# Splitting the mixer's weight units with ScalarE copies and an adding DMA in place of GpSimd

## The chip, the cores and the metric

The kernel runs on one core of a Trainium2 chip. The metric is device time in microseconds (us) of one execution; lower is better. One core has TensorE (matmuls; PE in the profile, its weight loads PEld), VectorE (DVE), ScalarE (ACT), GpSimd (POOL) and SyncE (SP, which here only issues DMAs).

## The reference

A decoder trunk of two layers over 512 tokens of width 1024, in float32:

```
for i in range(DEPTH):                                   # 2 layers
    h = 0.5 * swiglu(x, ffn1_w_gate[i], ffn1_w_up[i], ffn1_w_down[i])      # width 2752
    x = layer_norm(DEEPNORM_ALPHA * x + h, ...)
    h = hybrid_mixer(x, w_in[i], ..., w_out[i])
    x = layer_norm(DEEPNORM_ALPHA * x + h, ...)
    h = 0.5 * swiglu(x, ffn2_...)
    x = layer_norm(DEEPNORM_ALPHA * x + h, ...)
    x = x + sigmoid(x @ ple_w_gate[i] + ple_b_gate[i]) * (p[i] @ ple_w_proj[i])
```

The mixer projects x with w_in, runs three groups of attention heads and multiplies their concatenated outputs with w_out. The groups are: four NSA heads (a compressed branch over blocks of keys, and a window branch and a selected-block branch, which at 512 tokens are plain causal softmaxes), four differential heads (two causal softmaxes each, the second subtracted from the first with a factor), and eight FoX heads (a causal softmax with a decay term).

## The kernel before

**Split operands.** Every large product is made from split operands: a float32 matrix a is kept as hi + lo, where hi is a rounded to the reduced form (F32R) that TensorE multiplies in one pass, and lo = a - hi. A product then is three matmuls: hi·hi, hi·lo, lo·hi. Activations are split when they are made (`hilo`); weights are split on the fly.

**Weight units.** All weights lie in DRAM as one stream of units of 128x1024 floats (512 KB), in the order in which they are used. `_load` brings a unit into one of two raw buffers by a DMA on SyncE's queue (`opt["raw"]` is 2). `_split` makes two tiles: hi by a ScalarE copy (L218), and lo by a subtraction raw - hi (L219). The raw buffer is free for the next load when lo is done. The unit's tag, made in `unit_tags`, says which group of buffers holds hi and lo: "w" (six buffers), "p" or "h". A second letter P sends the subtraction to GpSimd instead of VectorE. The tag "wR" is for units used without a split.

**Which units go to GpSimd.** In each layer's mixer these are the sixteen projection units (`cmp`, `q0`, `q1`, `kk`, the four differential heads Gd0 to Gd3 and the eight FoX heads Gf0 to Gf7; tag "wP"), and six of the eight units of w_out (three "wP", three "pP"). With two layers that makes 44. All other units, 298 of them, are subtracted on VectorE.

**How far ahead.** `unit()` hands out a unit and calls `ahead`, which emits the split of the units up to two further on (`lead_mx` is 2). Their hi and lo need buffers, which come free when TensorE has finished with an earlier unit.

**The mixer's order.** The order of the steps is written by hand in the string `SEQ`. G is a head's projection, Q its scores and softmax (`softmax`: row maximum on VectorE at L733, exponential on ScalarE at L735, scaling by the reciprocal sum on VectorE at L743 or, for the second softmax of a differential head, L747), T the transposition on TensorE with the split of the result (L757, L241, L242), P the product with the values, W a piece of w_out. Within each engine the framework puts the instructions in its final order; it follows the program's order and its own reckoning of when each is ready.

**Names in the profile.** raw is a loaded unit, whi and wlo its two parts, ps a PSUM tile, P a softmax's matrix, sst its maxima and sums, oT the split output of a head pair, VF the FoX values, raw_r and rot the rotary embedding's tiles, gx and gy those of the compressed branch's activation function. L249 is the line of every matmul, L241 and L242 those of every activation split.

Of the kernel before, what the change touches and what calls it, by code (L numbers as in the profile page):

```python
# [19 lines left out]
F32 = mybir.dt.float32  # L20
F32R = mybir.dt.float32r
AF = mybir.ActivationFunctionType
ALU = mybir.AluOpType
# [144 lines left out]
class _Body:  # L168
    def __init__(self, tc, A, out, pools, opt):
        self.tc, self.nc, self.A, self.out, self.opt = tc, tc.nc, A, out, opt  # L170
        self.cp, self.rawp, self.sp, self.tp, self.mp, self.pp, self.Pp, self.op, self.dp = pools
        self.tags = unit_tags()
        self.dma_u = self.split_u = self.use_u = 0
        self.n_units = A["ws"].shape[0]
        self.rawt, self.hl = {}, {}
        self.lead = 3
        self.pending = []
        self.st = {}
# [29 lines left out]
    def _split(self, u):  # L208
        while self.dma_u <= u:
            self._load(self.dma_u)  # L210
            self.dma_u += 1
        r = self.rawt.pop(u)
        tag = self.tags[u]
        if tag.endswith("R"):
            self.hl[u] = r
            return
        hi, lo = self.big(tag[0], name="whi"), self.big(tag[0], name="wlo")
        self.nc.scalar.activation(hi, r, AF.Copy)  # L218
        (self.nc.gpsimd if self.opt["pool"] and tag[1:] else self.nc.vector).tensor_sub(lo, r, hi.bitcast(F32))  # L219
        self.hl[u] = hi, lo  # L220

    def ahead(self, n):
# [810 lines left out]
def unit_tags():  # L1033

    rest = 2 * NFULL + 1 + 2 * (NFULL // 2 + 1) - 3
    ffn = ["p"] * 3 + ["w"] * rest
    mix = ["p"] * 3 + ["w"]
    for n in SEQ:
        if n == "VF":
            mix += VFT  # L1040
        elif n[0] == "h":
            mix += [PHT[int(n[2])]]
        elif n[0] == "G" or n in ("cmp", "q0", "q1", "kk"):
            mix += ["w" if n in DVE_LO else "wP"]
    mix += ["wP"] * 3 + ["pP"] * 3 + ["w"] * 2
    ffn2 = ["h", "h", "h"] + ["w"] * rest
    ple = ["p"] * 2 + ["h"] * 8
    return (ffn + mix + ffn2 + ple) * L
# [50 lines left out]
```

## Time and profile before

| | |
|---|---|
| runs, median (lowest to highest of 3) | 2171.5 us (2169.47 to 2177.97) |
| the profiled execution's own time | 2160.23 us |
| its span, first to last instruction | 2158.5 us |
| TensorE busy | 2122.6 us (98%) |
| VectorE busy | 1034.2 us (48%) |
| ScalarE busy | 820.4 us (38%) |
| GpSimd busy | 151.5 us (7%) |

By stage, in us of the span:

| stage | length | TensorE busy | VectorE | ScalarE | GpSimd | granted clock |
|---|---|---|---|---|---|---|
| layer 1, first FFN (0 to 366) | 366 | 363.5 | 138.7 | 112.7 | 3.2 | 1.00 |
| layer 1, mixer (366 to 634) | 268 | 256.4 | 189.3 | 171.4 | 64.0 | 0.98 |
| end of w_out (634 to 670) | 36 | 35.7 | 30.5 | 12.4 | 4.0 | 1.00 |
| second FFN, embedding, next first FFN (670 to 1434) | 764 | 763.1 | 289.3 | 222.9 | 6.7 | 1.00 |
| layer 2, mixer (1434 to 1702) | 268 | 254.9 | 189.4 | 168.7 | 62.8 | 0.97 |
| the rest (1702 to the end) | 457 | 449.0 | 197.1 | 132.4 | 10.8 | 1.00 |

Matmuls are pipelined, so a stretch in which TensorE is busy all the time is not one in which it runs at its best rate; its idle time is a lower bound of what it loses. The granted clock is the share of TensorE's full clock that it had. The idle time of an engine that nobody waits for costs nothing.

### The profile page before, as it was taken

How to read it: one execution, taken by the hardware profiler on the slowest of the kernel's cores; microseconds unless marked ns; L12 is line 12 of the kernel's file. 1: busy time of each engine (PE TensorE's matmuls, PEld its weight loads, DVE VectorE, ACT ScalarE, POOL GpSimd, SP SyncE). 2: the span in 40 equal slices, each digit the busy share in tenths (PEclk: the TensorE clock that was granted, in tenths of full speed). 3: DMA queues.
4: the chain of work that ended last, by engine and by line, in shares of the span. 5: the costliest groups of instructions: out<-in, count | busy, mean ns of one | idle time of the engine just before them, and what ended most of it. 6: DMA issues, size and time to landing. Idle time of an engine off the chain costs nothing.

```text
span 2158.5 us, 25961 instructions
## 1 busy us (share of the span) xinstructions
PE 2122.6 (98%) x10135; PEld 1760.1 (82%) x10135; DVE 1034.2 (48%) x1777; ACT 820.4 (38%) x1372; POOL 151.5 (7%) x114
## 2 busy tenths in 40 slices
PE   9999999999999999999999999999999999999999
PEld 7888888787778888888888888887877788888877
DVE  4333336378875333335623333363788753333355
ACT  5222213457753222213422222143577532222132
POOL 0000001222220000000000000012212200000000
PEclk9999999999999999999999999999999999999999
DMA  6333334442341332334223323343323413333331
GB/s 205 97 98 98 108 107 154 128 149 77 111 154 59 98 98 97 116 100 129 96 67 95 95 97 106 109 161 120 123 94 103 163 60 98 97 98 116 99 129 67
DMA packets 76107, 236.07 MB, mean 109 GB/s; under 512 B 11344, under 2 KB 13520, under 8 KB 75984
## 3 DMA queue, kind: packets, MB, share of 16 engines
q1 hardware_dynamic: 74864, 230.74, 33.7%
q0 software_dynamic: 1120, 3.67, 0.4%
q8 instruction: 80, 1.31, 0.2%
q14 instruction: 43, 0.35, 0.0%
HBM read 209.46 MB, written 6.29 MB: 100 GB/s over the span
## 4 chain that ended last, share of the span: by engine, by line
PE 87%; DVE 6%; ACT 3%; DMA 2%; issue 1%; SPq 0%; DVEq 0%; ACTq 0%
PE ps L249 84%; PE ps L757 2%; DMA raw<-in_ws_dram 2%; ACT whi L218 1%; DVE wlo L219 1%; PE ps L266 1%; DVE P L733 0%; DVE P L743 0%; DVE x L303 0%; DVE P L747 0%; DVE oT L242 0%; ACT P L735 0%; DVE PT L242 0%; DVE raw_r L541 0%; DVE lnu L302 0%
## 5 line engine op out<-in xcount | busy, mean ns | idle before, releaser
L218 ACT ACTIVATE whi<-raw 128x1024 fp32r<-128x1024 f32 x342 | 362.0, 1060 | 1042.2 <-PE ps L249 674.0
L219 DVE TENSOR_TENSOR wlo<-raw,whi 128x1024 fp32r<-128x1024 f32 x298 | 363.9, 1223 | 606.4 <-ACT whi L218 605.8
L249 PE MATMUL ps<-xh,wlo 128*128 128x512 f32 (+1 forms) x1688 | 644.7, 382 | 0.0
L249 PE MATMUL ps<-xh,whi 128*128 128x512 f32 (+1 forms) x1688 | 643.7, 382 | 1.0 <-ACT xh L268 0.8
L249 PE MATMUL ps<-xl,whi 128*128 128x512 f32 (+1 forms) x1688 | 644.5, 382 | 0.0
L249 PE MATMUL ps<-whi,h 128*128 128x512 f32 x1376 | 427.2, 389 | 0.0
L249 PEld LDWEIGHTS ps<-xh,whi 128*128 128x128 f32 x1688 | 317.2, 188 | 61.0 <-ACT xh L268 1.5
L249 PEld LDWEIGHTS ps<-xh,wlo 128*128 128x128 f32 x1688 | 318.1, 188 | 58.5 <-DVE wlo L219 0.3
L249 PEld LDWEIGHTS ps<-xl,whi 128*128 128x128 f32 x1688 | 317.8, 188 | 58.8 <-DVE xl L269 0.6
L249 PEld LDWEIGHTS ps<-whi,h 128*128 128x128 f32 x1376 | 258.0, 188 | 53.1
L249 PE MATMUL ps<-wlo,h 128*128 128x512 f32 x704 | 274.1, 389 | 0.0
L335 DVE TENSOR_TENSOR hraw<-silu,ps 128x512 f32<-128x512 f32 x88 | 60.5, 688 | 291.5 <-PE ps L249 290.6
L249 PEld LDWEIGHTS ps<-wlo,h 128*128 128x128 f32 x704 | 132.1, 188 | 27.6
L219 POOL TENSOR_TENSOR wlo<-raw,whi 128x1024 fp32r<-128x1024 f32 x44 | 107.1, 2434 | 285.4 <-ACT whi L218 204.1
L735 ACT ACTIVATE P<-P,sst 128x128 f32<-128x128 f32 x192 | 106.5, 558 | 21.7 <-DVE sst L733 21.2
L249 PE MATMUL ps<-whi,xh 128*128 128x512 f32 (+2 forms) x264 | 99.3, 379 | 3.5 <-DVE VF L467 3.4
L298 POOL TENSOR_TENSOR mv<-mv,mhalf 128x1 f32<-128x1 f32 x24 | 23.0, 958 | 1099.6 <-DVE mv L297 1099.6
L249 PE MATMUL ps<-wlo,xh 128*128 128x512 f32 (+2 forms) x264 | 99.3, 377 | 0.0
L249 PE MATMUL ps<-whi,xl 128*128 128x512 f32 (+2 forms) x264 | 99.0, 376 | 0.0
L733 DVE CUSTOM_DVE_ANT_0 P<-ps,mask 128x128 f32<-128x128 f32 x192 | 88.9, 488 | 19.8 <-PE ps L249 16.7
L249 PE MATMUL ps<-whi,oT 128*128 128x512 f32 x256 | 86.0, 403 | 6.1 <-ACT oT L241 3.0
L242 DVE TENSOR_TENSOR PT<-ps,PT 128x512 fp32r<-128x512 f32 (+1 forms) x120 | 67.6, 592 | 14.6 <-ACT PT L241 14.1
(194 smaller groups left out, 1902.4 us busy)
## 6 DMA issues: line engine op xcount, KB each, us to landing
raw<-in_ws_dram SPq DMA_DIRECT2D x342, 512.0 KB
wraw<-in_ws_dram SPq DMA_DIRECT2D x16, 512.0 KB
dx<-x SPq DMA_DIRECT2D x8, 512.0 KB
x<-dx SPq DMA_DIRECT2D x8, 512.0 KB
rot<-raw_r SPq DMA_DIRECT2D x28, 128.0 KB
bc<-in_ln_g_dram SPq DMA_DIRECT2D x6, 512.0 KB
bc<-in_ln_b_dram SPq DMA_DIRECT2D x6, 512.0 KB
xraw<-in_xt_dram SPq DMA_DIRECT2D x8, 256.0 KB
```

The source lines that it names most:

```text
L218: self.nc.scalar.activation(hi, r, AF.Copy)
L219: (self.nc.gpsimd if self.opt["pool"] and tag[1:] else self.nc.vector).tensor_sub(lo, r, hi.bitcast(F32))
L242: nc.vector.tensor_sub(lo, src, hi.bitcast(F32))
L249: self.nc.tensor.matmul(out, l, r, start=start, stop=stop, skip_group_check=loose)
L266: nc.tensor.transpose(p[:, j], self.x[t][:, 128 * k:128 * k + 128], self.ident)
L298: nc.gpsimd.tensor_tensor(mv[:, 3:4], mv[:, 2:3], self.mhalf, op=ALU.pow)
L335: nc.vector.tensor_mul(r[0:n], s[up:up + n], pu[up:up + n])
L733: nc.vector.tensor_tensor_reduce(v, p[:, 0:n], self.mask[:, 512 - n:512], -scale, 3e38, ALU.add, ALU.min, nm[:, t:t + 1])
L735: nc.scalar.activation(v, v, AF.Exp, bias=nm[:, t:t + 1], scale=-1.0, accum_out=sm[:, t:t + 1])
L757: nc.tensor.transpose(p[:, 128 * i:128 * i + 128], P[:, off[t] + 128 * kb:off[t] + 128 * kb + 128], self.ident)
```

## The change

For a unit whose tag has the second letter P, lo is no longer raw - hi on GpSimd. ScalarE writes the negated raw, rounded to F32R as hi is, into lo, that is -hi; then a DMA issued by GpSimd adds raw to it in place. lo is then raw - hi, as before. The three "pP" units of w_out in each layer become "p", so VectorE subtracts them. So 38 units (19 a layer) go the new way, and six move from GpSimd to VectorE. Below the change the kernel's lines are five further down.

```diff
         hi, lo = self.big(tag[0], name="whi"), self.big(tag[0], name="wlo")
         self.nc.scalar.activation(hi, r, AF.Copy)
-        (self.nc.gpsimd if self.opt["pool"] and tag[1:] else self.nc.vector).tensor_sub(lo, r, hi.bitcast(F32))
+        if tag[1:]:
+
+            self.nc.scalar.activation(lo, r, AF.Copy, scale=-1.0)
+            self.nc.gpsimd.dma_start(lo.bitcast(F32), r, accum_op=ALU.add)
+        else:
+            self.nc.vector.tensor_sub(lo, r, hi.bitcast(F32))
         self.hl[u] = hi, lo
...
-    mix += ["wP"] * 3 + ["pP"] * 3 + ["w"] * 2
+    mix += ["wP"] * 3 + ["p"] * 3 + ["w"] * 2
```

## Rows read from the trace of the kernel before

**Rows 1.** Busy time of each engine in the two mixer stretches: the stretch, its length, then for PE, PEld, DVE, ACT and POOL the busy us and the number of instructions, the granted clock, the DMA engines' share and GB/s.

```profile
366.00:634.00 268.00, 256.44 (x1375) 211.11 (x1374) 189.26 (x488) 171.40 (x393) 64.00 (x42) 0.98 0.41 129
1434.00:1702.00 268.00, 254.88 (x1361) 210.50 (x1359) 189.44 (x485) 168.70 (x389) 62.82 (x43) 0.97 0.38 119
```

**Rows 2.** The waits of TensorE over the whole span: who waited, for whom, us in total, times, the longest.

```profile
PE ps L249 <- DVE sst L733: 6.5, 5, 2.4
PE ps L757 <- ACT P L735: 4.8, 2, 2.4
PE ps L249 <- DVE VF L467: 3.4, 2, 2.4
...
PE ps L249 <- DVE oT L242: 2.9, 2, 1.4
...
PE ps L713 <- DVE sc L706: 2.0, 2, 1.0
...
PE ps L249 <- DVE gx L648: 0.6, 1, 0.6
```

**Rows 3.** From timelines of VectorE and GpSimd in the mixers: start, duration, engine, line, operation, tiles, shape, how many are merged, and in brackets the engine's idle time before it and what ended it.

```profile
457.94 1.27 DVE L743 TENSOR_SCALAR P<-P,sst 128x128 f32<-128x128 f32 x4
478.64 3.09 DVE L743 TENSOR_SCALAR P<-P,sst 128x128 f32<-128x128 f32 x4
514.29 3.37 DVE L743 TENSOR_SCALAR P<-P,sst 128x128 f32<-128x128 f32 x4
512.02 0.69 DVE L242 TENSOR_TENSOR oT<-pair,oT 128x512 fp32r<-128x512 f32 x1
621.35 2.38 DVE L242 TENSOR_TENSOR oT<-pair,oT 128x512 fp32r<-128x512 f32 x1 [0.70 <-ACT oT L241]
620.82 2.36 POOL L219 TENSOR_TENSOR wlo<-raw,whi 128x1024 fp32r<-128x1024 f32 x1 [0.71 <-ACT whi L218]
391.24 2.51 DVE L541 TENSOR_TENSOR raw_r<-raw_r,rope 128x512 f32<-128x512 f32 x1 [2.46 <-DMA rot<-raw_r]
1463.83 2.73 DVE L541 TENSOR_TENSOR raw_r<-raw_r,rope 128x512 f32<-128x512 f32 x1 [2.62 <-DMA rot<-raw_r]
1467.19 2.77 DVE L543 TENSOR_TENSOR raw_r<-raw_r,rot 128x512 f32<-128x512 f32 x1
1540.88 3.27 DVE L645 TENSOR_SCALAR gy<-gy 128x64 f32<-128x64 f32 x1
```

**Rows 4.** From the page's costliest groups: the two parts of a weight unit's split, with count, busy us, mean ns of one, idle time before and what ended it.

```profile
L218 ACT ACTIVATE whi<-raw 128x1024 fp32r<-128x1024 f32 x342 | 362.0, 1060 | 1042.2 <-PE ps L249 674.0
L219 DVE TENSOR_TENSOR wlo<-raw,whi 128x1024 fp32r<-128x1024 f32 x298 | 363.9, 1223 | 606.4 <-ACT whi L218 605.8
...
L219 POOL TENSOR_TENSOR wlo<-raw,whi 128x1024 fp32r<-128x1024 f32 x44 | 107.1, 2434 | 285.4 <-ACT whi L218 204.1
```

**Rows 5.** Short stretches after waits of TensorE, columns as in rows 1; the granted clock is the third number from the end.

```profile
517.00:523.00 6.00, 5.08 (x25) 4.55 (x26) 5.49 (x17) 3.79 (x11) 0.70 (x2) 0.72 0.39 112
...
622.00:630.00 8.00, 6.57 (x22) 5.02 (x21) 5.72 (x6) 2.75 (x3) 1.18 (x1) 0.79 0.83 293
1472.00:1479.00 7.00, 6.59 (x22) 5.29 (x23) 0.95 (x2) 0.11 (x1) 0.00 (x0) 0.76 0.26 102
1544.00:1557.00 13.00, 12.77 (x55) 11.85 (x56) 7.30 (x29) 6.31 (x20) 0.10 (x1) 0.61 0.13 45
```

**Rows 6.** From the chain of work that ended last, the exponentials right behind the copy at 593.07 (start, us, what); and from the timelines of GpSimd and ScalarE around Gd3's split (columns as in rows 3).

```profile
594.40 1.91 ACT P L735 x6
...
537.20 2.40 POOL L219 TENSOR_TENSOR wlo<-raw,whi 128x1024 fp32r<-128x1024 f32 x1 [5.16 <-PE ps L249]
...
533.69 1.36 ACT L241 ACTIVATE PT<-ps 128x512 fp32r<-128x512 f32 x3
```

**Rows 7.** DMA issues: tiles, queue, operation, count, KB each, median us from issue to landing (for two kinds that GpSimd issues); and one load of a raw unit in the chain of work (start, us, what).

```profile
rope<-in_rope_dram POOLq DMA_DIRECT2D x8, 256.0 KB, 4.6
...
ptraw<-in_pt_dram POOLq DMA_DIRECT2D x4, 256.0 KB, 3.2
...
380.26 3.60 DMA raw<-in_ws_dram
```

**Rows 8.** From timelines, the split and the first use of lo: q1 in layer 1 (GpSimd's start, TensorE's first matmul with wlo), q1 in layer 2, Gf3 in layer 1 (ScalarE's copy, TensorE's first matmul with wlo), the third unit of w_out in layer 1.

```profile
428.53 2.40 POOL L219 TENSOR_TENSOR wlo<-raw,whi 128x1024 fp32r<-128x1024 f32 x1 [7.44 <-PE ps L249]
435.62 0.39 PE L249 MATMUL ps<-xh,wlo 128*128 128x512 f32 x1
1503.99 2.40 POOL L219 TENSOR_TENSOR wlo<-raw,whi 128x1024 fp32r<-128x1024 f32 x1 [7.44 <-PE ps L249]
1512.43 0.39 PE L249 MATMUL ps<-xh,wlo 128*128 128x512 f32 x1
441.36 1.05 ACT L218 ACTIVATE whi<-raw 128x1024 fp32r<-128x1024 f32 x1
452.22 0.48 PE L249 MATMUL ps<-xh,wlo 128*128 128x512 f32 x1
593.07 1.05 ACT L218 ACTIVATE whi<-raw 128x1024 fp32r<-128x1024 f32 x1
603.96 0.40 PE L249 MATMUL ps<-wlo,oT 128*128 128x512 f32 x1
```

**Rows 9.** The waits of SyncE's DMA queue over the whole span, columns as in rows 2.

```profile
SPq L205 <- POOL wlo L219: 146.6, 34, 17.4
```

## The prediction

> **What bounds the kernel now.** I read the busy time by stage first: in both mixer stretches TensorE is busy 256.4 and 254.9 of 268 us, VectorE about 189 (71%), ScalarE about 170 (64%), and the granted clock is 0.98 and 0.97; outside them TensorE stands at 98% or more with clock 1.00 (the table above). So the changed units lie in the only two stretches where TensorE has idle time to give back [rows 1]. Next, who TensorE waits for [rows 2]: the reader is to see that the waits on VectorE there add up to 6.5 + 3.4 + 2.9 + 2.0 + 0.6 = 15.4 us, and that the largest one on ScalarE, 4.8 us, is for the exponentials. Then why VectorE is late [rows 3]. The same four L743 operations take 1.27 us in one place, and 3.37 and 3.09 us where GpSimd's subtraction runs; one oT subtraction takes 0.69 us alone and 2.38 us beside a GpSimd subtraction that began 0.53 us earlier; rope's raw_r 2.51, 2.73 and 2.77 us; a 128x64 operation 3.27 us. The long oT ends 0.55 us after GpSimd's operation, about its own clean length: the two engines do not run such operations side by side, and the one that comes second stands still. Each of the long ones stands right before a TensorE wait of [rows 2].
>
> **What is removed.** 44 GpSimd subtractions of 2434 ns [rows 4], 22 a layer, and with them the hold on VectorE. GpSimd's own 107 us were no bound (7% of the span). Going through [rows 2] in order:
> - sst (the row maxima before a softmax), 6.5 us in 5 waits. Two are 1.8 each, behind the L743 run of 3.37 us and its twin in layer 2; the run loses 3.37 - 1.27 = 2.1, more than the wait. One of 2.4 follows the 3.27 us operation. Together 6.0; the two others are 0.2 each and are left.
> - VF, 3.4 us: 1.0 in layer 1, 2.4 in layer 2. Rope loses 2.51 - 0.68 = 1.8 in layer 1, and (2.73 + 2.77) - 2 x 0.68 = 4.1 in layer 2 (0.68 estimated from oT's 0.69, same shape). All could go, but in layer 1 ScalarE gets a second copy here (below), so 2.9.
> - sc, 2.0: the L743 run before it is late by 3.09 - 1.27 = 1.8 against 1.0 a layer: all 2.0.
> - gx, 0.6: gone.
> - oT at the end of the mixer, 2.9: the operation loses 1.7, but VectorE now subtracts for the last w_out unit at just this moment (1223 ns), so I take half, 1.4.
>
> Sum 12.9 us. TensorE that is early runs into waits that have not moved (the exponentials, 4.8), so I keep three quarters: **-9.7**. Bounds: 0, if every later wait takes it back, and 14.9.
>
> **The clock.** After four of these waits the granted clock is on its lower level, 1.2 instead of 2.4 GHz, for a while; the mean over each stretch is 0.72, 0.79, 0.76 and 0.61 [rows 5]. One minus the mean, times the length: 1.7, 1.7, 1.7 and 5.1 us, in sum 10.1. The one at 622 has a ScalarE wait in front of it too, and whether a shorter wait still drops the clock no row says. I take half, **-5.0**; bounds 0 and 10.1.
>
> **What is added on ScalarE.** 38 negated copies, 19 a layer, of the shape of L218's copies, 1060 ns [rows 4]: 40 us in all, in stretches where it is busy 64%. A copy delays what stands behind it until ScalarE's next idle moment; followed one by one through its queue, only two a layer reach the chain of waits. The unit at 593.07 has the exponentials of a differential head right behind it (1.91 us on the chain [rows 6]): 1.06 a layer, **+2.1**. The one before rope's q0 leaves about 0.5 us, taken off at VF above. The other seventeen are hidden by idle time of ScalarE waiting for TensorE or VectorE; without that cover all 38 cost 40. The negated copy doesn't wait for the first one, only for raw and for its buffer.
>
> **What is added on VectorE.** Six subtractions of 1223 ns, 7.3 us, in place of six GpSimd ones. The first of a layer comes earlier than GpSimd's (1.2 instead of 2.4), the second waits for a buffer while VectorE is idle, the third was counted at oT. Otherwise nothing.
>
> **What is added on the DMA.** 38 adding transfers on GpSimd's queue, each 512 KB of raw onto 512 KB in place. No row shows one. Before, lo stood about 3.5 us after the first copy began; now it stands after two copies (2.1) and D, the time from the issue to the landing. Lower bound for D: GpSimd's loads of 256 KB land after 3.2 to 4.6 us [rows 7]; upper bound: an add reads 1 MB and writes 512 KB, three times what such a load reads and writes, so 13.8 if all of the 4.6 grew with the bytes. The nearest is between GpSimd's 4.6 for half the bytes and the 3.6 of a raw load of 512 KB [rows 7]; I add about 2 for the second operand and take 6.5. The Trainium skill ("DMA: Bandwidth & Descriptors", Anatomy of one DMA — SWDGE (gpsimd) path) fits a GpSimd-issued DMA as 2.0 us plus bytes at 436 GB/s: an estimate of 3.2 us for 512 KB, 4.4 for two operands. For 256 KB that fit gives 2.6 where the rows have 3.2 and 4.6; by it the late term that follows is 0 instead of 0.5.
>
> Who waits for lo, in the tightest places [rows 8]: q1's buffer comes free at 428.53, its copy would end at 429.59, and TensorE reads lo at 435.62: margin 6.0; in layer 2 1512.43 - 1505.05 = 7.4. Gf3: 452.22 - (441.36 + 2.12) = 8.7. The third w_out unit: 603.96 - (593.07 + 2.12) = 8.8. Gf3 of layer 2 has 11.7; the third w_out unit there 8.8 again; all others have more. At D = 6.5 only q1 of layer 1 is late: **+0.5**.
>
> The raw buffer is also given back some 5 us later, so the load that waits for it stands longer at the head of SyncE's queue (146.6 us behind GpSimd now [rows 9]). Behind it wait rope's moves and those of the FoX heads, and for these the next head's scores. The raw itself has slack: at the tightest, Gd0's buffer is back at 461.05 + 2.1 + 6.5 = 469.7, the load takes 3.6, and the next copy from it begins at 476.15. **+1.0**, bounds 0 and 4 (a 2 us delay once a layer). GpSimd's other work (the copies at L788) has slack of several us.
>
> **Sum.** -9.7 - 5.0 + 2.1 + 0.5 + 1.0 = -11.1; the framework orders the queues anew, which I set at nothing. The profiled execution took 2160.2 us (span 2158.5), so 2149.1; it lay 11.3 below the median of the runs, 2171.5, and against that I forecast **2160.4**, 0.51% faster. A change under 0.5%, 10.9 us, can't be told from none.
>
> **Rivals.**
> *The add lands late.* Place: q1, Gf3 and the third w_out unit. With D above the margins the price is (D - 6.0) + (D - 8.7) + (D - 8.8) in layer 1 and (D - 7.4) + (D - 8.8) in layer 2: 5D - 39.7. The other terms are -11.6, so it decides from D = 10.3; at 13 (and 1.3 more for Gf3 of layer 2) it is 26.6, giving 2171.5 + 15.0 = 2186.5. For it: the add has three times the bytes of the load that took 4.6; against it: a raw load of 512 KB takes 3.6. Chance 0.13, of which 0.10 slower by over 0.5%.
> *ScalarE stands at the buffer.* GpSimd waited for lo's buffer behind the first copy; now ScalarE does, and what is queued behind the copy waits too. In layer 1 the waits were 3.8 (q1), 3.4 (537.20 after a copy that ended at 533.7 [rows 6]), 2.1 and 1.0 us; 20.6 over both layers. If all is on the path: -11.1 + 20.6 = +9.5, and with the copies of these units themselves, 1.06 each, four a layer, +18.0: 2189.5. It decides from 11.1 of these. For it: PT copies began right behind at 533.69. Against: at q1 ScalarE had nothing to do, and the framework can put ready work first. Chance 0.11, of which 0.08 slower.
> *The relief is swallowed, or doesn't come.* VectorE is early, but TensorE then waits for the exponentials, the clock falls anyway, and a GpSimd that issues transfers holds VectorE as its subtraction did. Terms: 0 + 0 + 2.1 + 0.5 + 1.0 = +3.6 at one end, half the gains (-3.7) at the other: 2168 to 2175. Chance 0.16, nearly all no change (0.02 faster).
> *The add waits for VectorE.* L743's runs and GpSimd's work exclude each other, and the order can turn: an issue behind a clean run starts 1.27 us late, D = 7.8, q1 late by 1.8 and 0.4: 2162. Chance 0.04, no change. The Trainium skill states that as a trap ("SBUF — State Buffer", SBUF: two separate sides): while VectorE runs a two-port operation, GpSimd cannot write descriptors. No run here shows it yet.
>
> **Range and chances.** Forecast, 0.56; its own range 2150 (nearly all waits kept) to 2168: 0.42 faster by over 0.5%, 0.14 not. If both the waits and the clock come back whole and cost nothing, 14.9 + 10.1 = 25: 2146.5, the low end. The high end takes in the slower rivals up to D = 13: 2186. Faster 0.42 + 0.02 = 0.44; slower 0.10 + 0.08 = 0.18; the rest, 0.38, the same.
>
> **What the profile after would show.** A run of four L743 operations at 1.3 us and oT at 0.7; TensorE's waits on sst, VF, sc and gx gone; fewer stretches under clock 1.00; ScalarE 40 us busier; no TensorE wait for lo. Wrong would be: a wait of matmuls on the adding DMA, exponentials late behind copies, or the same clock.

## Result and the profile after

| | median of the runs | its runs | profiled execution: time, span, TensorE busy |
|---|---|---|---|
| before | 2170.5 us | 2169.4 to 2178.0 (4) | 2160.2, 2158.5, 2122.6 us |
| after | 2149.2 us | 2147.4 to 2155.9 (4) | 2147.4, 2145.7, 2116.4 us |

The changed kernel is faster: 0.9909 of the time before, 95% interval [0.9888, 0.9930]. Two later comparisons with more runs give less: 0.9939 [0.9923, 0.9955] and 0.9949 [0.9924, 0.9973], medians 12.6 and 13.2 us apart. Profile against profile it is 12.8 us; the profiled execution of after is the fastest of its four, that of before is faster than all four of its row.

First the two mixer stretches, columns as in [rows 1], whose answer this is:

```profile
366.00:634.00 268.00, 256.23 (x1390) 210.43 (x1389) 180.86 (x495) 189.12 (x412) 27.66 (x39) 0.99 0.62 167
1434.00:1702.00 268.00, 260.28 (x1404) 214.68 (x1403) 183.63 (x499) 190.70 (x414) 28.19 (x40) 0.99 0.61 168
```

In the same 268 us TensorE gets through 15 and 43 more matmuls, with the clock at 0.99. ScalarE is 18 and 22 us busier, GpSimd 36 and 35 less, and the DMA engines' share rises from 0.41 and 0.38 to 0.62 and 0.61. Then TensorE's waits over the whole span, the answer to [rows 2]:

```profile
PE ps L762 <- ACT P L740: 4.7, 2, 2.3
...
PE ps L254 <- DMA fa<-fa: 2.5, 2, 2.1
PE ps L254 <- ACT fb L566: 1.7, 2, 0.9
...
PE ps L254 <- DVE VF L472: 1.3, 1, 1.3
...
PE ps L254 <- DMA wraw<-in_ws_dram: 1.3, 1, 1.3
...
PE ps L254 <- DMA fa<-ct: 0.7, 2, 0.3
PE ps L254 <- DVE sst L738: 0.4, 2, 0.2
```

The five waits on VectorE that made up 15.4 us are down to 2.0 (VF 1.3, sst 0.4, and 0.3 for g, where gx was). In their place stand some new ones: 2.5 + 0.7 for moves of the FoX heads and 1.3 for a weight load, all issued by SyncE, 1.7 for a ScalarE result (fb), and 0.9 for VectorE's osq. No matmul waits for an add. Whole span: TensorE's idle time went from 2158.5 - 2122.6 = 35.9 us to 2145.7 - 2116.4 = 29.3, 6.6 less, and its busy time fell by 6.2 with the same 10135 matmuls; less busy time for the same matmuls is the clock's part.

Why VectorE is no longer late is read from its groups kept apart by shape (line, operation, shape, count | busy us, mean ns of one | idle before). Three groups of before, with all their instructions, then the same ones of after:

```profile
L242 DVE TENSOR_TENSOR oT<-pair,oT 128x512 fp32r<-128x512 f32 x16 | 14.9, 929 | 2.1 <-ACT oT L241 2.1
...
L541 DVE TENSOR_TENSOR raw_r<-raw_r,rope 128x512 f32<-128x512 f32 x14 | 13.5, 961 | 12.8 <-DMA rot<-raw_r 12.8
...
L743 DVE TENSOR_SCALAR P<-P,sst 128x128 f32<-128x128 f32 x16 | 8.2, 511 | 0.3
```

```profile
L247 DVE TENSOR_TENSOR oT<-pair,oT 128x512 fp32r<-128x512 f32 x16 | 11.0, 687 | 0.7 <-ACT oT L246 0.7
...
L546 DVE TENSOR_TENSOR raw_r<-raw_r,rope 128x512 f32<-128x512 f32 x14 | 9.6, 686 | 16.0 <-DMA rot<-raw_r 9.4 <-ACT whi L218 6.7
...
L748 DVE TENSOR_SCALAR P<-P,sst 128x128 f32<-128x128 f32 x16 | 4.5, 283 | 0.3
```

The long ones of [rows 3] are gone from the mean: 929 to 687 ns, 961 to 686, 511 to 283. GpSimd's subtraction did not hold every operation of VectorE, though. In before, PT<-ps,PT (128x512), which reads PSUM, took 687 ns at the median in the 17 cases beside one and 681 in the other 63; rope's raw_r<-raw_r,rope, all in SBUF, took 2.51 and 2.73 us beside one and 0.69 in the other 12. So what the change frees are VectorE's operations within SBUF.

The split's own parts, the answer to [rows 4] and [rows 7] (the last line is a DMA issue: count, KB each, median us from issue to landing):

```profile
L221 ACT ACTIVATE wlo<-raw 128x1024 fp32r<-128x1024 f32 x38 | 40.1, 1055 | 7.3 <-PE ps L254 7.3
...
L222 POOL DMA_DIRECT2D wlo<-raw x38 | 33.2, 874 | 316.0 <-ACT wlo L221 238.2 <-PE ps L809 25.4 <-ACT gy L649 19.9
...
wlo<-raw POOLq DMA_DIRECT2D x38, 512.0 KB, 5.0
```

An add lands 5.0 us after its issue (4.4 to 7.6), and the issue takes GpSimd 0.87 us. SyncE's loads behind such units wait about as long as before, the answer to [rows 9]:

```profile
SPq L205 <- DMA wlo<-raw: 133.3, 29, 10.8
```

### The profile page after: what moved, and what is told of

Read it like the earlier page. It is cut to its first block, busy times and chain, and to the rows that moved or that the text cites. A ratio compares the mean times of both kernels' runs of the same rounds, so it can differ in the third digit from the quotient of the medians.

```text
span 2145.7 us, 26020 instructions
## 1 busy us (share of the span) xinstructions
PE 2116.4 (99%) x10135; PEld 1754.9 (82%) x10135; DVE 1008.9 (47%) x1783; ACT 854.2 (40%) x1410; POOL 78.5 (4%) x108
## 5 line engine op out<-in xcount | busy, mean ns | idle before, releaser
L224 DVE TENSOR_TENSOR wlo<-raw,whi 128x1024 fp32r<-128x1024 f32 x304 | 371.9, 1224 | 611.9 <-ACT whi L218 606.6
L762 PE MATMUL ps<-ident,P 128*128 128x128 f32 x400 | 64.6, 282 | 6.1 <-ACT P L740 4.7
L246 ACT ACTIVATE PT<-ps 128x512 fp32r<-128x512 f32 (+1 forms) x120 | 58.5, 523 | 16.1 <-PE ps L762 12.4
```

Of the source, the lines that this page charges most:

```text
L224: self.nc.vector.tensor_sub(lo, r, hi.bitcast(F32))
L246: nc.scalar.activation(hi, src, AF.Copy)
L762: nc.tensor.transpose(p[:, 128 * i:128 * i + 128], P[:, off[t] + 128 * kb:off[t] + 128 * kb + 128], self.ident)
```

## Experiments

The kernels ran in three sets, each on a chip of its own together with runs of before; so a kernel's time is compared with before of its own set, and times across sets are good for a rough comparison only. Each execution comes with its span and mean granted clock. I split the mean over a kernel's executions in two: span times (1 - clock), what the clock's lower level took, and the rest of the span. The clock is given to three places, so one execution's split is good to 1 us. The rest is the steadier part: before has 2145.5, 2146.2 and 2145.5 in the three sets, and 16.1, 20.5 and 16.7 lost to the clock.

| kernel | median, us | ratio to before, 95% interval | lost to the clock | the rest |
|---|---|---|---|---|
| first set: before | 2163.0 (26 runs) | | 16.1 | 2145.5 |
| before, built again | 2168.1 (10) | 1.0027 [1.0004, 1.0049] | 18.6 | 2147.5 |
| after | 2150.3 (10) | 0.9939 [0.9923, 0.9955] | 8.8 | 2140.1 |
| after, GpSimd reading again | 2177.7 (5) | 1.0071 [1.0043, 1.0098] | 16.5 | 2159.4 |
| only w_out's six units | 2163.5 (10) | 0.9983 [0.9955, 1.0011] | 15.6 | 2142.4 |
| second set: before | 2168.5 (15) | | 20.5 | 2146.2 |
| only ScalarE's second copies | 2171.3 (10) | 1.0010 [0.9998, 1.0023] | 12.8 | 2156.5 |
| all 44 by the adding DMA | 2159.0 (6) | 0.9954 [0.9937, 0.9970] | 8.6 | 2148.3 |
| the add issued twice | 2224.3 (4) | 1.0255 [1.0230, 1.0280] | 38.9 | 2183.2 |
| cmp, kk, q1 on VectorE | 2146.9 (4) | 0.9900 [0.9882, 0.9918] | 7.0 | 2138.0 |
| third set: before | 2164.1 (27) | | 16.7 | 2145.5 |
| after | 2150.9 (12) | 0.9949 [0.9924, 0.9973] | 10.6 | 2139.5 |
| cmp, kk, q1 on VectorE | 2146.3 (6) | 0.9918 [0.9887, 0.9949] | 3.6 | 2139.6 |
| and Gf0, Gf1 | 2147.2 (10) | 0.9924 [0.9902, 0.9947] | 4.7 | 2140.9 |
| all 44 on VectorE | 2172.9 (12) | 1.0043 [1.0022, 1.0064] | 28.2 | 2142.2 |

**The measure itself: before, built again, and after.** No edit.

> The kernel before once more, for a second profile of it. If its profiled execution (2160.2 us, 11 below the median of its runs) was a lucky one, this one shows a span of 2165 to 2175 and more of TensorE's half clock than the 27 us of the first; if the first was typical for the code, 2157 to 2161 with the same six stretches of half clock.

> The changed kernel once more. 2147 to 2152 us timed; a profile that differs from its first by a stretch of half clock at most (3.4 us of it cost 1.7 us).

The same kernel built again differs from itself by 0.27% and its interval leaves out 1. So a single difference of under about 0.3%, 6 us, is not told from none here. Of the change's 12.6 us in this set, 7.3 are the clock's and 5.4 the rest; in the third set 6.1 and 6.0.

**Bring the hold back without the subtraction's result.** After each add GpSimd also computes raw - hi, into a tile that nobody reads (scr, scrp in the profile):

```diff
-            self.nc.gpsimd.dma_start(lo.bitcast(F32), r, accum_op=ALU.add)
+            d = self.nc.gpsimd.dma_start(lo.bitcast(F32), r, accum_op=ALU.add)
+            for c in (slice(0, 512), slice(512, 1024)): self.after(self.nc.gpsimd.tensor_sub(self.scr, r[:, c], hi.bitcast(F32)[:, c]), d)
...
-        nc.vector.memset(self.mhalf, -0.5)
+        nc.vector.memset(self.mhalf, -0.5); self.scr = self.cp.tile([128, 512], F32, name="scrp")
```

> The changed kernel, and GpSimd also subtracts, into a scratch tile, for the same 38 units right after it has issued the add. lo does not depend on it. Theory (GpSimd's subtraction held VectorE): the waits on sst, VF and sc come back, about 11 us of the 15 in the first profile of before, with half clock behind them: 2160 to 2172 us. Rival (the framework's new order of the queues made the gain): the order is nearly that of the changed kernel, so 2147 to 2153. Rival (the six units moved to VectorE made it): 2147 to 2155 too.

The gain is gone and more: 27 us over the changed kernel, and 5.7 over the highest time that was expected. VectorE's and GpSimd's groups by shape in this kernel:

```profile
L548 DVE TENSOR_TENSOR raw_r<-raw_r,rot 128x512 f32<-128x512 f32 x14 | 14.7, 1051 | 0.2
...
L546 DVE TENSOR_TENSOR raw_r<-raw_r,rope 128x512 f32<-128x512 f32 x14 | 13.3, 953 | 14.9 <-DMA rot<-raw_r 14.9
...
L645 DVE TENSOR_TENSOR gy<-gx 128x64 f32<-128x64 f32 x4 | 4.2, 1054 | 0.0
...
L222 POOL TENSOR_TENSOR scrp<-raw,whi 128x512 f32<-128x512 f32 x76 | 113.6, 1495 | 2.8
```

Two of rope's operations are at 0.95 and 1.05 us instead of 0.69, one of 128x64 at 1.05, and TensorE waits 6.7 us for sst (0.4 in after) and 3.3 for sc (none in after). No other engine uses what GpSimd computes here, so it is GpSimd's running that does this, and not the queues' order, which the rival would have kept. Nor is it the raw buffer: SyncE's loads wait 137.1 us for adds here and 133.3 in after, TensorE 0.4 for an add. The hold falls on other operations than in before: oT (128x512) and L748's 128x128 operations are at their clean lengths here, 686 and 283 ns on the mean, so the wait on sst has come back by other operations. Why it overshoots stays open. VectorE is held no longer than in before: without its weight subtractions it is busy 30.0 us more than in after, before 33.3 us more. The Trainium skill ("SBUF — State Buffer", SBUF: two separate sides) calls the ports that VectorE and GpSimd share an exclusive lock, held for a whole instruction. The rows agree: oT 929 ns on the mean before and 687 after.

**One part alone: w_out's six units.** The kernel before with the new tags.

```diff
-    mix += ["wP"] * 3 + ["pP"] * 3 + ["w"] * 2
+    mix += ["wP"] * 3 + ["p"] * 3 + ["w"] * 2
```

> Only the tags of w_out's six units are changed; the 38 others are subtracted by GpSimd as before. Theory: what this part gives is the oT wait at the end of each mixer, 1.4 to 2.9 us in all, and perhaps a stretch of half clock (1.7): 2165 to 2170 us. Rival (the six units made most of the gain): 2150 to 2158.

In its trace the wait on oT at VectorE (2.9 us) is gone, and sst (9.2), VF (3.1) and sc (2.0) remain. That is the step "oT" by itself. Its time, 0.5 us over before and 4.6 under before built again, can't be told from none; it lies 1.5 under the range expected. Its rest is 3.1 us under before's (2142.4 against 2145.5), as much as the wait that went (2.9), and more than half of after's 5.4.

**The other part alone: all 44 units by the adding DMA.** w_out's last three stay "pP".

```diff
-    mix += ["wP"] * 3 + ["p"] * 3 + ["w"] * 2
+    mix += ["wP"] * 3 + ["pP"] * 3 + ["w"] * 2
```

> All 44 units go the new way, w_out's last three of a layer as well (they stay pP). Theory: the first of them is needed at once (before, GpSimd's lo ended at 611.28 and TensorE reads the unit from 611.0); copy, copy and add end 7.1 us after the first copy began at 607.76, so 3 to 4 us late in each layer, and half clock behind that: 2155 to 2164. Rival (it doesn't matter who makes the last three): 2147 to 2153.

It is 9.5 us under before of its set, three quarters of the whole change's 12.6 and 13.2, and all of it is the clock's (20.5 to 8.6 us); the rest is 2.1 over before. TensorE waits 4.8 us for whi and 2.0 for VectorE's wlo at the end of w_out, which neither kernel does. One line of ScalarE there, with its idle time:

```profile
640.28 2.19 ACT L218 ACTIVATE whi<-raw 128x1024 fp32r<-128x1024 f32 x2 [8.69 <-DMA raw<-in_ws_dram]
```

Three units in a row on the add keep both raw buffers, the next two loads are late, and with them w_out's last units. So the two parts of the change need each other: by the rest, 2148.3 against after's 2140.1 and 2139.5 in the other sets, VectorE's three subtractions a layer are worth some 8 us once the others go by DMA. After did not run in this set, so that is a comparison across sets.

**The second copies alone.** The kernel before, with ScalarE's negated copy into lo ahead of GpSimd's subtraction, which overwrites it; units tagged "wP" only.

```diff
+        if tag == "wP": self.nc.scalar.activation(lo, r, AF.Copy, scale=-1.0)
         (self.nc.gpsimd if self.opt["pool"] and tag[1:] else self.nc.vector).tensor_sub(lo, r, hi.bitcast(F32))
```

> The kernel before, and ScalarE also writes the negated copy into lo for the 38 units; GpSimd's subtraction then overwrites it. So ScalarE's part of the change is there, the hold on VectorE stays, no add. Theory (the copies fall into ScalarE's idle time but for the one before the exponentials): 2 us more without the clock's part, 2165 to 2171 timed. Rival (ScalarE is nearly the bound, 40 us of copies show): 2180 or more.

In sum they cost 2.8 us, which the interval can't tell from none: 38 copies don't cost 40. But this is a net of two things, 10.3 us more of the rest and 7.7 less of the clock's, since the framework orders the queues anew and other waits come up (gy 7.3 us, and x at 4.7 where before has 2.6). So it excludes the 29 us that the rival adds (20.6 of waits and 8.5 of copies) and does not measure the copy's own price. It also shows that the clock's part doesn't follow the hold alone: GpSimd subtracts here as before, and 7.7 us less are lost to the clock.

**How late may the add be?** It is issued twice, so lo is 2 raw - hi.

```diff
             self.nc.gpsimd.dma_start(lo.bitcast(F32), r, accum_op=ALU.add)
+            self.nc.gpsimd.dma_start(lo.bitcast(F32), r, accum_op=ALU.add)
```

> The changed kernel with the add of raw issued twice, the second waiting for the first; lo is then 2 raw - hi, which is not the split. lo lands about 10 us after the first issue instead of 5. Theory (margins of 6.0, 7.4, 8.7 and 8.8 at q1, Gf3 and the third w_out unit): 5 x 10 - 39.7 = 10 us of waits for lo, and the raw buffers and SyncE's queue 5 us later on top: 2158 to 2170. Rival (the framework's order hides a later lo): within 3 of the changed kernel.

Measured: 55.8 us over before of its set, so some 70 over after, about seven times the waits that were expected. TensorE's waits in this kernel:

```profile
PE ps L254 <- DMA wlo<-raw: 17.9, 10, 3.2
PE ps L254 <- DVE sst L738: 10.7, 8, 4.4
PE ps L254 <- ACT raw_r L543: 6.6, 2, 3.5
PE ps L254 <- DMA fa<-ct: 5.7, 2, 5.1
PE ps L254 <- ACT fb L566: 5.6, 4, 3.1
PE ps L254 <- ACT whi L218: 4.4, 3, 2.4
```

Only 17.9 us are lo itself, in ten places where I had counted five. Of the others, some stand behind a raw load in SyncE's queue, which issues in order; I followed one of them. The queue there (start, us, what):

```profile
590.08 0.48 SPq L558 DMA_DIRECT2D fb<-fb  x1
595.09 0.33 SPq L205 DMA_DIRECT2D raw<-in_ws_dram  x1
595.51 1.15 SPq L558 DMA_DIRECT2D fa<-ct  x1
```

The load stands until 595.09 for a buffer that the add still reads, the move of fa behind it is issued at 595.51, and the product that needs it starts at 600.35, 3.5 us late (the profile names no releaser for this wait; that it is the move goes by the order). That all the others have this cause is not shown. The second part is the clock: 38.9 us lost to it, against 8.8 and 10.6 in after. So, across sets, some 43 us are in the rest and 28 to 30 are the clock's.

**Units back to VectorE: three, then five.** Twice, the second time beside after and a version with two more.

```diff
-DVE_LO = ()
+DVE_LO = ("cmp", "kk", "q1")
```

> The changed kernel, but cmp, kk and q1 are subtracted by VectorE, which is busy 9 of 40 us there (400 to 440). Their raw buffers come back about 5 us earlier, so SyncE's queue is free for the FoX heads' moves. Theory: the waits on fa (2.1 and 0.5 us) and on wraw (1.3) of the changed kernel go: 2145 to 2148. Rival (those waits have another cause, and VectorE's 3.7 us more per layer show): 2150 or more.

> The changed kernel once more, beside the two versions below on one chip. Theory and rival alike: 2147 to 2152 us, 0.7 to 1.0% under the kernel before.

> cmp, kk and q1 split by VectorE, the other 32 units by the adding DMA. In the first look at it TensorE's wait for q0's moves (fa<-fa, 2.1 and 0.5 us) was gone, but it waited 1.1 and 0.9 us for Gf3's lo on the add. Theory: the moves wait at SyncE behind loads whose buffer the adds give back late, and VectorE's own split gives it back earlier, so it is 2 to 3 us under the changed kernel: 2145 to 2149. Rival: the difference between the two was one of the two calls they ran in; then they are within 1 us.

```diff
-DVE_LO = ()
+DVE_LO = ("cmp", "kk", "q1", "Gf1", "Gf0")
```

> Gf0 and Gf1 go back to VectorE as well, so 28 units are left on the adding DMA. Theory: Gf3's buffer and rope's q0 no longer stand behind ScalarE's second copies, so the waits on VF (1.3 us) and on Gf3's add (1.0 us a layer) go too: 1 to 3 us under the version with three, 2143 to 2147. Rival: VectorE is late again in rope and the values of the FoX heads, where it has 2.4 us of subtractions more a layer: 0 to 4 us over the version with three.

Beside after, in the third set, the version with three is 4.6 us faster, and the two intervals overlap; in the second set, without after beside it, it has 0.9900 of before's time, where after had 0.9939 and 0.9949 in its sets. So it beats before, and after by no more than the same kernel differs from itself. In the first of its two traces the waits for fa<-fa and for the weight load are gone; in the second 0.9 us of fa<-fa is left. But in the third set, beside after, its rest is that of after (2139.6 and 2139.5) and all of the difference is the clock's, so "the moves get through sooner" is not what I can show as its cause. With five units TensorE waits 4.1 us for VF (2.3 with three, 1.3 in after): VectorE is late again in the FoX values, as the rival said, at a price (0.9 us) that the runs can't tell from none.

**No add at all: VectorE does everything.** The kernel before, with tags that have no second letter.

```diff
-            mix += ["w" if n in DVE_LO else "wP"]
-    mix += ["wP"] * 3 + ["pP"] * 3 + ["w"] * 2
+            mix += ["w"]
+    mix += ["w"] * 3 + ["p"] * 3 + ["w"] * 2
```

> All 44 units by VectorE: no GpSimd, no adding DMA, no negated copies. VectorE has 38 x 1.22 = 46 us more than in the changed kernel, ScalarE 40 less. Theory: what made the kernel before slow is GpSimd's hold on VectorE, and an equal time of VectorE's own work at an equal place costs about the same as the hold did: its 44 GpSimd operations of 2.43 us gave VectorE some 15 us of TensorE's waits, and 54 us of its own subtractions at 71% busy give 10 to 20 us of them; 2155 to 2168, so the adding DMA is worth most of the gain. Rival: VectorE's 29% of idle time covers it and the adding DMA wins nothing: 2147 to 2152, as the changed kernel.

No faster than before, and 22 us over after: the adding DMA is worth the whole gain. But not by the theory's path: the rest is only 2.7 us over after (2142.2 against 2139.5), so VectorE covers its 46 us almost as the rival said, and it is the clock that takes 28.2. TensorE does wait for gy, 2.34 and 2.37 us, once a layer. In VectorE's timeline two weight subtractions, 2.44 us, stand among the operations before gy:

```profile
493.93 0.69 DVE L700 TENSOR_TENSOR sc<-sc,cmx 128x512 f32<-128x512 f32 x1
494.54 1.22 DVE L219 TENSOR_TENSOR wlo<-raw,whi 128x1024 fp32r<-128x1024 f32 x1
...
495.81 1.22 DVE L219 TENSOR_TENSOR wlo<-raw,whi 128x1024 fp32r<-128x1024 f32 x1
```

For the clock, one stretch of this kernel (columns as in [rows 1]):

```profile
467.00:484.00 17.00, 17.00 (x77) 16.21 (x76) 5.21 (x19) 3.64 (x9) 0.00 (x0) 0.50 0.19 52
```

TensorE is busy for all of 17.00 us, waits for nobody, and runs at half clock. Nor did it wait before that: from 436 to 486 it is idle for 0.12 us in all, and the clock falls twice there. What it did before the first fall is in its timeline, 46 matmuls on 32 columns with one other between them:

```profile
443.08 2.76 PE L249 MATMUL ps<-xs,wraw 128*128 128x32 f32 x24
445.68 0.48 PE L249 MATMUL ps<-PT,VF 128*128 128x512 f32 x1
446.00 4.16 PE L249 MATMUL ps<-xs,wraw 128*128 128x32 f32 x22
```

24 of them take 2.76 us, the next 22 take 4.16: the clock fell there (granted 1.00 from 443 to 446, 0.58 from 446 to 450). Whether that order of work brings the long stretches is open: after itself has one of 17 us at the same point of layer 2 in two of its three profiled executions, and none in the other, with the same program and the same order:

```profile
1521.00:1538.00 17.00, 17.00 (x75) 16.11 (x74) 7.61 (x23) 6.97 (x20) 1.25 (x2) 0.50 0.64 201
```

```profile
1511.00:1528.00 17.00, 17.00 (x138) 16.17 (x137) 11.85 (x32) 11.44 (x28) 1.25 (x2) 1.00 0.81 258
```

The first is after in the third set, the second the profiled execution shown at the top, whose layer 2 stands some 3 us earlier. So that execution is one in which the clock did well.

## Why the prediction was right, and where it was not

**Direction and sum: right, the sum in part by luck.** The sum was -11.1 us; the measured differences are 12.8 (profile to profile), 12.6 and 13.2 (medians with ten and more runs a side).

**The forecast time, 2160.4, was 11 too high.** The mechanism is not what this comes from; the term that was mis-sized is the base. The sum gave 2149.1 against the profiled execution; I then added the 11.3 us by which that execution lay below the median of three runs, 2171.5. 68 more runs of before had medians of 2163.0, 2168.5 and 2164.1. Of these runs 14 lie below the profiled 2160.2 and 9 above 2171.5, so neither was in the middle; the second profile of before came out as was expected if the first was a lucky one (span 2169.7, 21.7 us of it lost to the clock where the first lost 15.1). From 2164 the same sum gives 2153. The remaining few us are the size of what the same kernel differs from itself. The first comparison's 21 us is partly this as well: before's four runs in it had a median of 2170.5. At 2149.2 the time lies in the range given, and 0.8 under the likeliest case's own.

**Waits: the net was right (-6.1 forecast, -6.6 in idle time, -5.4 and -6.0 in the rest), two terms in it were not.** VectorE's waits went by 13.4, a little more than the 12.9 counted, though rope's layer-1 VF wait stayed (1.0 before, 1.3 after), where 0.5 was to be left. The quarter that I gave back to later waits did not come: exponentials 4.8 before, 4.7 after. What came instead is SyncE's queue: fa<-fa, fa<-ct and the weight load, 4.5 us, where I had 1.0 and a bound of 4. The two errors cancel, and that is luck. Of the 5.4 and 6.0 us, w_out's six units by themselves bring 3.1, so the 38 others bring some 2 to 3 on top of them. The experiment with two adds points to this as the sensitive term.

**ScalarE's copies: the term (+2.1) did not come as forecast.** I put the delay on the exponentials. The framework put the second copy behind them, and the wait for them stayed (4.8 before, 4.7 after). A new wait, 1.7 us in both layers together, is on fb, behind a second copy in ScalarE's queue. ScalarE's timeline in layer 1, and the matmul that waits (0.84 us here, 0.85 in layer 2):

```profile
598.11 1.05 ACT L221 ACTIVATE wlo<-raw 128x1024 fp32r<-128x1024 f32 x1
...
600.59 1.36 ACT L246 ACTIVATE PT<-ps 128x512 fp32r<-128x512 f32 x3 [0.82 <-PE ps L762]
601.82 0.62 ACT L566 ACTIVATE fb<-ps 128x512 fp32r<-128x512 f32 x1
...
602.50 0.50 PE L254 MATMUL ps<-whi,oT 128*128 128x512 f32 x1 [0.84 <-ACT fb L566]
```

Between the copy and fb ScalarE stands idle for 0.82 us, waiting for TensorE; by the prediction's own rule the copy's delay ends there. And the version without any second copy, all on VectorE, waits 3.3 us for fb. So the 1.7 is not shown to be the copies' price; more likely it belongs to the new order of the queues, which I had set at nothing. That it is near 2.1 is luck.

**The add: D = 5.0 where I took 6.5** (4.4 to 7.6 within one execution). q1's lo was in time here; other executions of after show 0.4 and 1.5 us of TensorE waiting for an add. The Trainium skill ("DMA: Bandwidth & Descriptors", Anatomy of one DMA — SWDGE (gpsimd) path) gave the estimate of 4.4 for two operands: the shortest add measured is that, the median is above it.

**The clock: -5.0 forecast, -7.3 and -6.1 measured** (busy time -6.2). Half of the four stretches was a guess inside its bounds, and its reason, that the clock falls after these waits, is not shown to be what makes this part. With the hold gone, the version all on VectorE lost 11.5 us more to the clock than before; with the hold kept, the second copies alone lost 7.7 less. So the waits account for the half of the gain that is in the rest, 5.4 and 6.0, and the cause of the clock's half stays open. Nor can it be had from one trace: the lost share differs between executions of one program, as the two stretches above do.

**The rivals.** *The add lands late* did not happen, but its formula, 5D - 39.7, was wrong: two adds in a row make some 10 us, for which it gives about 11, and it cost some 70. It counted lo's own readers and left out the queue behind the raw buffer; so it would decide below the 10.3 that I gave, how far no run shows. *ScalarE stands at the buffer*: ScalarE was idle 7.3 us in all before the second copies in after, where the rival had 20.6, and all copies alone cost 2.8 us in sum, 10.3 in the rest. *The relief is swallowed*: excluded, by the clock and the idle time both; a GpSimd that issues adds doesn't hold VectorE as its subtraction did. Of rope's 14 sums raw_r<-raw_r,rot, within SBUF and 836 ns on the mean before, the 4 that ran beside an issue took 686 ns at the median, the other 10 took 687. *The add waits for VectorE*: the 38 issues took 851 to 1055 ns, so no sign of 1.27 us more.

## What to carry over

When two engines exclude each other, price the waits behind the one that is held, not the busy time of the one that holds. When a buffer is given back later, follow the load that waits for it through its queue to everything behind it: in the experiment with two adds everything else together was dearer than the late operand itself. And lay a sum on as many runs of the kernel before as there are; three runs put the base 7.5 us off, more than any term of the sum but one.

## What the runs showed of the hardware

GpSimd's subtraction within SBUF can hold VectorE's operations that work within SBUF alone (rope's took 2.51 to 2.77 us beside it and 0.69 else), and did not hold those that read PSUM (687 ns beside it, 681 else). An adding DMA of 512 KB within SBUF, issued by GpSimd, lands after 5.0 us at the median and costs GpSimd 0.87 us; two in a row on one tile are too slow for this kernel, at some 70 us. TensorE's clock can be at its lower level, 1.2 GHz, for 17 us with TensorE busy in all of them and idle for 0.12 us of the 31 before, so a clock loss does not need a wait in front of it; in the all-VectorE version it took 28 us of the span against 10.6 in after, for 2.7 us more of everything else.
